# Last convolution rows and the samples' normaliser transposed on TensorE and moved by rows; GpSimd begins the sample states' transfers

## The chip, the cores and the metric

The kernel runs on one core of one Trainium2 chip. The metric is the device time of one execution in microseconds (us); for the kernel before, the median of 3 runs is 2701.5 us. The engines of the core are called PE (TensorE), ACT (ScalarE), DVE (VectorE), POOL (GpSimd) and SP (SyncE, which here only begins transfers).

## What is computed

One inference step of a single decoder layer, for one prompt of 2048 tokens and for 8 samples of one token each, model width 1024. Two mixers stand side by side: a gated delta rule (4 heads, 128 x 128 states) behind a causal convolution of width 4, and an mLSTM (4 heads, 64 x 128 matrix states with a normaliser vector and a running maximum).

```python
def _layer(x, states, params):
    h = _rmsnorm(x, norm_pre_mix)
    mix, new_states = _mixer(h, conv_buf, S0, C0, n0, m0, w_in, conv_w, ...)
    x = x + _rmsnorm(mix, norm_post_mix)
    u = jnp.square(jax.nn.relu(_rmsnorm(x, norm_pre_mlp) @ w_up))
    x = x + _rmsnorm(u @ w_down, norm_post_mlp)
    return x, new_states

# in _mixer
    (gq, gk, gv, gz, gb, ga, mq, mk, mv, mo, mi, mf) = _split(h @ w_in, IN_SPLITS)
    qkv, conv_new = _causal_conv(concatenate([gq, gk, gv]), conv_buf, conv_w)   # conv_new: the last 3 rows before the convolution
    o_gdn, S_new = _gated_delta_rule(gq, gk, gv, g, beta, S0, chunk)
    h_ml, C_new, n_new, m_new = _mlstm(mq, mk, mv, ig, lf, C0, n0, m0, chunk)
    return o @ w_out, (conv_new, S_new, C_new, n_new, m_new)

# one step for a sample
    S = exp(g) * S + k (beta * (v - exp(g) * S^T k))^T
    C = w_prev * C + p * k v^T;   n = w_prev * n + p * k
```

Besides the tokens' outputs, the new states are outputs: for the prompt the last three convolution rows (`o_pconv`, 3 x 1536), S, C, n and m; for the samples the same, among them `o_sS` (8 x 4 x 128 x 128), `o_sC` (8 x 4 x 64 x 128) and `o_sn` (8 x 4 x 64).

## The kernel before

The prompt is worked through in four segments of 512 tokens (`SEG`); the 8 samples (`NB`) ride as extra columns with segment 1 (`SS`). Activations lie channel-major: channels on the 128 partitions, tokens along the free axis. Every large product is a list of half units (`Half`): four weight blocks of 128 x 128 against four activation blocks, each in three passes (lines 195, 196, 200), 12 matmuls in all. The weights of a half unit come in one transfer of 256 KB into one of four buffers `wraw` (L171), ACT casts them to the high part `whl` (L178), DVE forms the low part (L183). PE writes into the banks `bk`, from which ACT or DVE take the results: in the up products, ACT takes them to `tB` (L1232, three buffers), which also holds the convolution's results before they are stored to `dqkv` (L309).

`play()` goes through the list `main`, which fixes the order of the half units; between them it takes steps from generators ("streams"): the mixers of a segment (`mixer`), the norms (`norm_mid`, `final`), and the samples' work (`sample_mix`, `sample_states`). A `yield` with a number says how much of the large products goes by before the next step. A scheduler then orders the instructions of each engine by its own estimate of the times, so an instruction whose inputs are early may be moved ahead of its place in the program. Each engine works in order; SP's queue is in order too, so a transfer that waits for its source or its place holds back all that SP would begin after it.

All transfers are begun by SP (`Q.dma_start`). Those that the change touches are these.

- `mixer(3)` ends by storing the prompt's states. The three last rows of the convolution lie in `halo` (128 channels x 12 tiles x 3 rows). Three transfers (L1067) move one row each, and in each the neighbours in DRAM lie on different partitions: 1536 separate words.
- `sample_mix` reads the mLSTM states of the samples, two heads at a time, into tiles `Ct` of 130 columns: 128 of C, column 128 for the normaliser n, column 129 zero. C comes in rows of 128 words, n word by word (L959: 64 partitions x 8 samples, one word each). PE then multiplies all 130 columns (L965).
- `sample_states`, a stream beside the last segment's up and down products, updates the samples' states. For each of four heads it loads S (`st_S`, 512 KB), loads the update broadcast to all partitions (`dUs`, 512 KB), multiplies and adds on POOL (L1014 to L1016), and stores `o_sS`. For each of two pairs of mLSTM heads it loads C, n and the values broadcast (`dvs`), works on all 130 columns on POOL (L1033 to L1035), and stores C and n, n again word by word (L1040). The tiles are the two buffers `xt`.

The stream `final` of segment 2 (POOL line 1306) runs before `sample_states`; the last products' sums of squares (POOL line 1124) and the last norm come after it.

Of the kernel before, what the change touches and what calls it, by code (L numbers as in the profile page):

```python
# [24 lines left out]
def program(tc, ctx, d, T):  # L25
# [48 lines left out]
    pairsum = const([128, 16], "pairsum")  # high and low part of each gate, added  # L74
# [8 lines left out]
    # the first rows, and a place for each of them normalised  # L83
# [3 lines left out]
    gain = const([128, 4, 8], "gain")  # channel-major: before and after the mixing, before and after the MLP  # L87
# [138 lines left out]
    def norm_a(xt, n, xs=None):  # L226
        """rows / rms"""
# [8 lines left out]
    def norm_b(rows, n, col, gain, halves, bank):  # L236
        """the rows of some token tiles, n tokens in all, to channel-major, times the gain, in two parts"""
# [96 lines left out]
    def a_units(s, halves, order=range(28)):  # L334
# [25 lines left out]
        if s == 0:  # L360
            # the first three of them by token halves, while the second half is being normalised
# [6 lines left out]
    def log1p_exp(L, ab, shape_n):  # L368
        """L = log1p(exp(-ab)), ab >= 0."""
# [15 lines left out]
    def gates(s):  # L385
# [32 lines left out]
        cum = sb([128, 2, 2, 16], "cum", 1)  # (cumulated | chunk total) x (g | lf)  # L418
# [69 lines left out]
    gstate = {}  # L488

    def decay(src, bias, n):  # L490
        """exp(src[c] + bias[s]) for s <= c, else 0: rows s, columns c, four heads"""
# [14 lines left out]
    def gdn_half(s, hf, D):  # L506
# [78 lines left out]
        # inverses of the 32 x 32 diagonal blocks, one block to a partition  # L585
# [62 lines left out]
        # the recurrence over chunks  # L648
# [47 lines left out]
    def out_T(s, n, on, base):  # L696
        """normalised heads, gate and gain, to channel-major scratch."""
# [84 lines left out]
    def sample_mix(s):  # L782
# [3 lines left out]
        # convolution with the buffered rows  # L786
# [39 lines left out]
        # gates, along the free axis on every partition and (last column) along the partitions  # L826
# [45 lines left out]
        # gated delta rule  # L872
# [57 lines left out]
        # mLSTM  # L930
# [21 lines left out]
        Cts = []  # L952
        for j in range(2):
            Ct = sb([128, NB, 130], "xt", 2)
            V.memset(Ct[:, :, 129:130], 0.0)
            for h2 in range(2):
                rows = slice(64 * h2, 64 * h2 + 64)
                Q.dma_start(Ct[rows, :, 0:128], d["st_C"][:, 2 * j + h2].rearrange("b k v -> k b v"))
                Q.dma_start(Ct[rows, :, 128:129], d["st_n"][:, 2 * j + h2].rearrange("b (k o) -> k b o", o=1))  # L959
# [41 lines left out]
        later.update(eg=eg, kn=kn, dU=dU, wp=wp, pp=pp, dv=dv)  # L1001
# [3 lines left out]
    def sample_states():  # L1005
        eg, kn, dU, wp, pp, dv = (later[k] for k in ("eg", "kn", "dU", "wp", "pp", "dv"))
        for h in range(4):
            St = sb([128, NB, 128], "xt", 2)
            Q.dma_start(St, d["st_S"][:, h].rearrange("b k v -> k b v"))
            Ub = sb([128, NB, 130], "xt", 2)  # L1010
            Q.dma_start(Ub[:, :, 0:128], dU[8 * h:8 * h + 8].partition_broadcast(128))
            bs = [128, NB, 128]
            yield 3
            G.tensor_tensor(St, St, eg[:, 8 * h:8 * h + 8].unsqueeze(2).broadcast_to(bs), op=ALU.mult)  # L1014
            G.tensor_tensor(Ub[:, :, 0:128], Ub[:, :, 0:128], kn[:, 8 * h:8 * h + 8].unsqueeze(2).broadcast_to(bs), op=ALU.mult)
            G.tensor_tensor(St, St, Ub[:, :, 0:128], op=ALU.add)  # L1016
            yield 4
            Q.dma_start(d["o_sS"][:, h].rearrange("b k v -> k b v"), St)
            yield 2
        for j in range(2):  # L1020
            Ct = sb([128, NB, 130], "xt", 2)
            vb = sb([128, NB, 130], "xt", 2)
            G.memset(Ct[:, :, 129:130], 0.0)
            G.memset(vb[:, :, 128:130], 1.0)
            for h2 in range(2):
                rows = slice(64 * h2, 64 * h2 + 64)
                Q.dma_start(Ct[rows, :, 0:128], d["st_C"][:, 2 * j + h2].rearrange("b k v -> k b v"))
# [546 lines left out]
```

## Time and profile before

| | before |
|---|---|
| median of 3 runs | 2701.5 us (2699.88 to 2704.51) |
| profiled execution, span from the first to the last instruction | 2703.2 us (its time; nothing is shown around it) |
| PE / DVE / ACT / POOL busy | 2605.9 / 1730.3 / 1284.0 / 412.8 us |
| packets on the DMA queue of SP | 319040, 374.57 MB |
| mean granted clock of TensorE | 0.989 |

PE is busy for 96% of the span, so the time of the kernel is the time of its matmuls and of the few gaps between them. A stretch is read by three things: how long PE is busy in it, how many matmuls it does, and which clock it was granted. The next question at a gap is which instruction ended it, and what that one had waited for.

### The profile page before, as it was taken

To read this page: it belongs to the slowest core of one execution; us is meant where nothing else is said; L and a number is where in the kernel's file an instruction comes from. 1 tells how busy PE (TensorE), PEld (TensorE's weight loads), DVE (VectorE), ACT (ScalarE), POOL (GpSimd) and SP (SyncE) were. 2 spreads that over 40 slices of the span, in tenths; PEclk is the share of its full clock that TensorE was granted. 3 is DMA by queue.
4 is the path that set the end of the run, shared out by engine and by line. 5 is a ranking of instruction groups with operands and counts; after the bars stand their busy time and mean duration, and the time that the engine had idled before them with its cause. 6 is when DMAs were issued, how large, how long until landed. Compare 5 with 4: busy or idle time off the path is not lost.

```text
span 2703.2 us, 44345 instructions
## 1 busy us (share of the span) xinstructions
PE 2605.9 (96%) x15907; PEld 2271.5 (84%) x15907; DVE 1730.3 (64%) x3508; ACT 1284.0 (48%) x3119; POOL 412.8 (15%) x470
## 2 busy tenths in 40 slices
PE   8999999999999999999799999999999999978998
PEld 6889999778888788878699999997787888766887
DVE  6765768647757557765575865587667567754445
ACT  5636457435535345644455354465363455422332
POOL 2101012311000002420000000062000004430002
PEclk9999999999999999999899999999999999999999
DMA  4444457553323245744433243454242346664222
GB/s 167 156 150 141 145 165 224 193 160 133 102 92 122 99 152 171 238 165 141 97 99 117 95 152 111 153 180 144 88 129 98 123 146 205 205 149 105 94 96 84
DMA packets 319261, 377.41 MB, mean 140 GB/s; under 512 B 53289, under 2 KB 177129, under 8 KB 319033
## 3 DMA queue, kind: packets, MB, share of 16 engines
q1 hardware_dynamic: 319040, 374.57, 44.0%
q8 instruction: 126, 2.06, 0.3%
q14 instruction: 95, 0.77, 0.1%
HBM read 314.04 MB, written 60.53 MB: 139 GB/s over the span
## 4 chain that ended last, share of the span: by engine, by line
PE 83%; DMA 6%; DVE 5%; issue 2%; ACT 2%; POOL 1%; SPq 1%; DVEq 0%; ACTq 0%; POOLq 0%
PE bk L195 25%; PE bk L196 25%; PE bk L200 24%; DVE whl L183 2%; DMA wraw<-w_o 1%; DMA xt<-x_prompt 1%; DVE nt L1197 1%; DMA wraw<-w_up 1%; DVE X L1201 1%; PE mx L563 1%; ACT whl L178 1%; DMA xt<-dO 1%; DMA dqkv<-tB 1%; PE mx L655 1%; PE mx L770 1%
## 5 line engine op out<-in xcount | busy, mean ns | idle before, releaser
L178 ACT CAST whl<-wraw 128x512 fp32r<-128x512 f32 x872 | 539.2, 620 | 972.6 <-PE bk L200 828.6
L183 DVE TENSOR_TENSOR whl<-wraw,whl 128x512 fp32r<-128x512 f32 (+1 forms) x872 | 646.5, 744 | 490.3 <-ACT whl L178 476.1
L195 PE MATMUL bk<-Y,whl 128*128 128x512 f32 (+2 forms) x2208 | 733.2, 346 | 5.7 <-ACT whl L178 3.8
L196 PE MATMUL bk<-Y,whl 128*128 128x512 f32 (+2 forms) x2208 | 731.4, 345 | 0.0
L195 PE MATMUL bk<-X,whl 128*128 128x512 f32 (+3 forms) x2024 | 659.1, 342 | 46.4 <-ACT whl L178 31.8
L196 PE MATMUL bk<-X,whl 128*128 128x512 f32 (+3 forms) x2024 | 656.6, 341 | 2.7 <-DVE X L1201 2.5
L200 PE MATMUL bk<-Y,whl 128*128 128x512 f32 (+2 forms) x2176 | 488.3, 344 | 8.8 <-DVE whl L183 8.8
L195 PEld LDWEIGHTS bk<-Y,whl 128*128 128x128 f32 x2208 | 415.8, 188 | 60.8 <-ACT whl L178 5.9
L195 PEld LDWEIGHTS bk<-X,whl 128*128 128x128 f32 x2024 | 384.1, 190 | 91.7 <-ACT whl L178 35.3
L196 PEld LDWEIGHTS bk<-Y,whl 128*128 128x128 f32 x2208 | 416.7, 189 | 50.3
L200 PE MATMUL bk<-X,whl 128*128 128x512 f32 (+3 forms) x2024 | 442.5, 339 | 8.3 <-DVE whl L183 8.2
L196 PEld LDWEIGHTS bk<-X,whl 128*128 128x128 f32 x2024 | 384.3, 190 | 47.6 <-DVE X L1201 4.1
L200 PEld LDWEIGHTS bk<-Y,whl 128*128 128x128 f32 x2176 | 358.9, 189 | 62.1 <-DVE whl L183 11.5
L200 PEld LDWEIGHTS bk<-X,whl 128*128 128x128 f32 x2024 | 326.6, 189 | 54.1 <-DVE whl L183 11.4
L1245 DVE TENSOR_TENSOR acc<-acc,bk 128x512 f32<-128x512 f32 (+2 forms) x296 | 164.1, 556 | 151.8 <-PE bk L200 147.7
L1124 POOL TENSOR_TENSOR NQ<-NQ,nt 128x256 f32<-128x256 f32 (+4 forms) x145 | 142.8, 988 | 499.0 <-ACT nt L1123 492.1
L1234 DVE TENSOR_TENSOR tB<-tB 128x512 f32<-128x512 f32 (+1 forms) x160 | 93.8, 588 | 55.7 <-ACT Y L1233 54.7
L305 DVE SCALAR_TENSOR_TENSOR tB<-tA,cw,tB 128x512 f32<-128x512 f32 x144 | 107.9, 750 | 13.7 <-ACT tB L301 11.0
L1235 DVE TENSOR_TENSOR Y<-tB,Y 128x512 fp32r<-128x512 f32 (+1 forms) x160 | 97.6, 612 | 3.2
L1232 ACT ACTIVATE tB<-bk 128x512 f32<-128x512 f32 (+1 forms) x160 | 81.7, 511 | 29.2 <-DMA dqkv<-tB 13.1
L1233 ACT ACTIVATE Y<-tB 128x512 fp32r<-128x512 f32 (+1 forms) x160 | 87.3, 549 | 4.3
L596 DVE TENSOR_TENSOR W<-xt 32x30 f32<-32x30 f32 (+14 forms) x240 | 76.2, 317 | 20.0 <-DMA xt<-dn 15.2
(380 smaller groups left out, 2456.4 us busy)
## 6 DMA issues: line engine op xcount, KB each, us to landing
wraw<-w_dn SPq DMA_DIRECT2D x264, 256.0 KB, 2.6
wraw<-w_up SPq DMA_DIRECT2D x256, 256.0 KB, 2.6
wraw<-w_a SPq DMA_DIRECT2D x224, 256.0 KB, 2.8
wraw<-w_o SPq DMA_DIRECT2D x128, 256.0 KB, 3.5
dqkv<-tB SPq DMA_DIRECT2D x48, 256.0 KB, 2.8
gb<-drb SPq DMA_DIRECT2D x32, 256.0 KB, 3.9
qk<-dqkv SPq DMA_DIRECT2D x16, 512.0 KB, 3.7
dzo<-tB SPq DMA_DIRECT2D x32, 256.0 KB, 3.2
```

The costliest lines, as they stand in the source:

```text
L178: A.copy(self.hl[:, 0], self.raw)
L183: V.tensor_tensor(lo, raw, hi.bitcast(F32), op=ALU.subtract)
L195: PE.matmul(o, lhsT=w, rhs=acts[:, k, 0, c0:c1], start=(self.first and k == 0), stop=False)
L196: PE.matmul(o, lhsT=w, rhs=acts[:, k, 1, c0:c1], start=False, stop=(self.packed and self.last and k == 3))
L200: PE.matmul(o, lhsT=w, rhs=acts[:, k, 0, c0:c1], start=False, stop=(self.last and k == 3))
L305: V.scalar_tensor_tensor(acc, pre[:, t:t + SEG], cw[:, j, t:t + 1], acc, op0=ALU.mult, op1=ALU.add)
L1124: G.tensor_tensor(total[:, c0:c1], total[:, c0:c1], sq[:, c0:c1], op=ALU.add)
L1232: A.activation(r[:, :n], p[:, :n], AF.Relu)
L1233: A.activation(sl[:, 0, c0:c1], r[:, :n], AF.Square)
L1234: V.tensor_tensor(r[:, :n], r[:, :n], r[:, :n], op=ALU.mult)
L1235: V.tensor_tensor(sl[:, 1, c0:c1], r[:, :n], sl[:, 0, c0:c1].bitcast(F32), op=ALU.subtract)
L1245: V.tensor_tensor(a, a, p[:, :c1 - c0], op=ALU.add)
```

## The change

Three edits; besides, comments are dropped, which shifts the line numbers by up to 17.

1. The prompt's last convolution rows: DVE copies `halo` into `t36` (128 x 36, tile name `hrow`), PE transposes it to 36 rows of 128 channels, ACT copies these out of PSUM into `rows36` (in the buffer `gb`), and one transfer stores 36 rows of 512 B.
2. The samples' normaliser: `sample_mix` loads n as 8 rows of 256 words (`nr`), PE transposes them into `nT` (128 x 2 x 8), which is kept, and DVE copies its columns into `Ct`. `sample_states` updates `nT` on POOL with instructions of 8 columns, and at its end PE transposes `nT` back, DVE copies the rows out, and one transfer stores `o_sn`. The tiles of the second pass have 128 columns instead of 130, so POOL's two memsets for each go.
3. In `sample_states` the transfers of the states and of the broadcasts are begun by POOL (`G.dma_start`), not by SP: 4 x 3 + 2 x 6 = 24 of them.

```diff
 # sample_mix
         pc = mx()
         Cts = []
+        nr = sb([128, 512], "on", 2)[:NB, :256]
+        Q.dma_start(nr, d["st_n"].rearrange("b h k -> b (h k)"))
+        p = mx()
+        for j in range(2):
+            PE.transpose(p[:, j * NB:(j + 1) * NB], nr[:, j * 128:(j + 1) * 128], ident[:NB, :NB])
+        nT = const([128, 2, NB], "nT")
+        V.tensor_copy(nT, p[:, 0:2 * NB].rearrange("p (a b) -> p a b", a=2))
         for j in range(2):
             Ct = sb([128, NB, 130], "xt", 2)
             V.memset(Ct[:, :, 129:130], 0.0)
+            V.tensor_copy(Ct[:, :, 128:129], nT[:, j].unsqueeze(2))
             for h2 in range(2):
                 rows = slice(64 * h2, 64 * h2 + 64)
                 Q.dma_start(Ct[rows, :, 0:128], d["st_C"][:, 2 * j + h2].rearrange("b k v -> k b v"))
-                Q.dma_start(Ct[rows, :, 128:129], d["st_n"][:, 2 * j + h2].rearrange("b (k o) -> k b o", o=1))
...
 # sample_states
         for h in range(4):
-            St = sb([128, NB, 128], "xt", 2)
-            Q.dma_start(St, d["st_S"][:, h].rearrange("b k v -> k b v"))
-            Ub = sb([128, NB, 130], "xt", 2)
-            Q.dma_start(Ub[:, :, 0:128], dU[8 * h:8 * h + 8].partition_broadcast(128))
-            bs = [128, NB, 128]
+            St = sb([128, 1040], "xt", 2)[:, :1024].rearrange("p (a b) -> p a b", a=NB)
+            G.dma_start(St, d["st_S"][:, h].rearrange("b k v -> k b v"))
+            Ub = sb([128, 1040], "xt", 2)[:, :1024].rearrange("p (a b) -> p a b", a=NB)
+            G.dma_start(Ub, dU[8 * h:8 * h + 8].partition_broadcast(128))
             yield 3
             G.tensor_tensor(St, St, eg[:, 8 * h:8 * h + 8].unsqueeze(2).broadcast_to(bs), op=ALU.mult)
...
-            Q.dma_start(d["o_sS"][:, h].rearrange("b k v -> k b v"), St)
+            G.dma_start(d["o_sS"][:, h].rearrange("b k v -> k b v"), St)
             yield 2
         for j in range(2):
...
-            G.memset(Ct[:, :, 129:130], 0.0)
-            G.memset(vb[:, :, 128:130], 1.0)
             for h2 in range(2):
                 rows = slice(64 * h2, 64 * h2 + 64)
-                Q.dma_start(Ct[rows, :, 0:128], d["st_C"][:, 2 * j + h2].rearrange("b k v -> k b v"))
-                Q.dma_start(Ct[rows, :, 128:129], d["st_n"][:, 2 * j + h2].rearrange("b (k o) -> k b o", o=1))
+                G.dma_start(Ct[rows], d["st_C"][:, 2 * j + h2].rearrange("b k v -> k b v"))
                 o0 = (2 * j + h2) * 8
-                Q.dma_start(vb[rows, :, 0:128], dv[o0:o0 + 8].partition_broadcast(64))
+                G.dma_start(vb[rows], dv[o0:o0 + 8].partition_broadcast(64))
...
             G.tensor_tensor(Ct, Ct, vb, op=ALU.add)
+            G.tensor_tensor(nT[:, j], nT[:, j], wp[:, j], op=ALU.mult)
+            G.tensor_tensor(nT[:, j], nT[:, j], pp[:, j], op=ALU.add)
             yield 4
             for h2 in range(2):
                 rows = slice(64 * h2, 64 * h2 + 64)
-                Q.dma_start(d["o_sC"][:, 2 * j + h2].rearrange("b k v -> k b v"), Ct[rows, :, 0:128])
-                Q.dma_start(d["o_sn"][:, 2 * j + h2].rearrange("b (k o) -> k b o", o=1), Ct[rows, :, 128:129])
+                G.dma_start(d["o_sC"][:, 2 * j + h2].rearrange("b k v -> k b v"), Ct[rows])
             yield 2
+        p = mx()
+        for j in range(2):
+            PE.transpose(p[:NB, j * 128:(j + 1) * 128], nT[:, j], ident)
+        nr = sb([128, 512], "on", 2)[:NB, :256]
+        V.tensor_copy(nr, p[:NB, 0:256])
+        Q.dma_start(d["o_sn"].rearrange("b h k -> b (h k)"), nr)
+        yield
 # mixer(3), at its end
             Q.dma_start(d["o_pm"], mlast)
-            for r in range(3):
-                Q.dma_start(d["o_pconv"][r].rearrange("(j p o) -> p j o", p=128, o=1), halo[:, :, r:r + 1])
+            t36 = sb([128, 36], "hrow", 1)
+            V.tensor_copy(t36[:, :].rearrange("p (r j) -> p j r", r=3), halo)
+            p = mx()
+            PE.transpose(p[:36, 0:128], t36, ident)
+            rows36 = sb([128, 512], "gb", 1)[:36, :128]
+            A.copy(rows36, p[:36, 0:128])
+            Q.dma_start(d["o_pconv"].rearrange("r (j p) -> (r j) p", p=128), rows36)
             yield
```

The order in which the engines take their instructions moves at three places. The first is SP's queue around `o_pconv`. Before, the scheduler has put the three stores far ahead of the end of `mixer(3)`, to where `halo` is complete, in the up products of segment 1; `dqkv` is the convolution's output, `gb<-drb` a broadcast of gates.

```order
525 L309 DMA dqkv_132<-tB 128x512
526 L171 DMA wraw<-w_up 128x512 x2
527 L309 DMA dqkv_132<-tB 128x512
528 L1067 DMA o_pconv<-halo 128x12x1
529 L171 DMA wraw<-w_up 128x512
530 L1067 DMA o_pconv<-halo 128x12x1 x2
531 L171 DMA wraw<-w_up 128x512
532 L502 DMA gb<-drb_151 128x512
533 L309 DMA dqkv_132<-tB 128x512
```

After the change the store needs a bank of PSUM and the buffer `gb`, which come round at the end of `mixer(3)`; it stands in SP's queue there, among the loads of the output projection's weights (`w_o`).

```order
747 L1075 DMA o_pC<-C 64x2x128
748 L1076 DMA o_pn<-C 64x2x1
749 L1075 DMA o_pC<-C 64x2x128
750 L1076 DMA o_pn<-C 64x2x1
751 L699 DMA on<-dzo_140 128x4x128
752 L171 DMA wraw<-w_o 128x512 x2
753 L1084 DMA o_pconv<-gb 36x128
754 L704 DMA dO_144<-on 128x4x128
755 L171 DMA wraw<-w_o 128x512 x2
```

So the store has moved from the middle of segment 1's up products to the first output weights of segment 3, some 220 rows later on SP. The second place is SP's queue during `sample_states`; before, loads and stores of the states stand between the weight loads.

```order
819 L1018 DMA o_sS<-xt 128x8x128
820 L1027 DMA xt<-st_C 64x8x128
821 L1028 DMA xt<-st_n 64x8x1
822 L171 DMA wraw<-w_dn 128x512
823 L1027 DMA xt<-st_C 64x8x128
824 L1030 DMA xt<-dvs 64x8x128
825 L1028 DMA xt<-st_n 64x8x1
826 L171 DMA wraw<-w_dn 128x512
827 L1030 DMA xt<-dvs 64x8x128
828 L171 DMA wraw<-w_dn 128x512 x2
829 L171 DMA wraw<-w_up 128x512
830 L1039 DMA o_sC<-xt 64x8x128
```

After the change, the same stretch of SP's queue, from the last store of `final` on, holds weight loads and one store of `o_sn`.

```order
792 L1328 DMA o_yT<-xt 128x2x512
793 L171 DMA wraw<-w_dn 128x512 x5
794 L171 DMA wraw<-w_up 128x512 x3
795 L1052 DMA o_sn<-on 8x256
796 L171 DMA wraw<-w_up 128x512 x5
797 L171 DMA wraw<-w_dn 128x512 x8
```

All that is left of the states on SP is that store. The third place is POOL, where the states' arithmetic follows the last additions of `final`; before, it is arithmetic alone.

```order
276 L1306 TENSOR_TENSOR xt<-xt,nt 128x512 x8
277 L1014 TENSOR_TENSOR xt<-xt,seg 128x1024
278 L1015 TENSOR_TENSOR xt<-xt,sy 128x8x128
279 L1016 TENSOR_TENSOR xt<-xt 128x1024
280 L1014 TENSOR_TENSOR xt<-xt,seg 128x1024
```

After, POOL also begins the transfers, in the order of the code.

```order
278 L1323 TENSOR_TENSOR xt<-xt,nt 128x512 x8
279 L1018 DMA xt<-st_S 128x8x128
280 L1020 DMA xt<-dUs 128x1024
281 L1022 TENSOR_TENSOR xt<-xt,seg 128x1024
282 L1023 TENSOR_TENSOR xt<-xt,sy 128x1024
283 L1024 TENSOR_TENSOR xt<-xt 128x1024
284 L1026 DMA o_sS<-xt 128x8x128
285 L1018 DMA xt<-st_S 128x8x128
```

POOL's 24 transfers now stand between the last addition of `final` and the first addition to the last sum of squares (L1141, which was L1124), and the first load of S can no longer begin before the last of those additions has been taken up.

## Rows read from the trace of the kernel before

**Rows 1.** The page, part 1: busy us of each engine (share) x instructions.

```profile
PE 2605.9 (96%) x15907; PEld 2271.5 (84%) x15907; DVE 1730.3 (64%) x3508; ACT 1284.0 (48%) x3119; POOL 412.8 (15%) x470
```

**Rows 2.** Timeline of PE, 1346 to 1358 us: start, us, what [idle before, releaser].

```profile
1346.47 0.58 PE L195 MATMUL bk<-X,whl 128*128 128x260 f32 x1 [12.62 <-ACT tB L1232]
...
1351.20 0.58 PE L195 MATMUL bk<-X,whl 128*128 128x260 f32 x1 [1.76 <-ACT tB L1232]
...
1353.97 0.42 PE L195 MATMUL bk<-X,whl 128*128 128x260 f32 x1
...
1355.74 0.28 PE L195 MATMUL bk<-X,whl 128*128 128x260 f32 x1
...
1357.17 1.60 PE L563 MATMUL mx<-xs 128*128 128x256 f32 x12
```

**Rows 3.** Waits, 1305 to 1352 us: us in total, times, longest us.

```profile
ACT tB L1232 <- DMA dqkv<-tB: 13.1, 1, 13.1
```

**Rows 4.** Timeline of SP, 1305 to 1352 us: start, us, what.

```profile
1315.56 1.18 SPq L1067 DMA_DIRECT2D o_pconv<-halo  x2
1317.21 12.87 SPq L171 DMA_DIRECT2D wraw<-w_up  x1
...
1330.65 0.38 SPq L309 DMA_DIRECT2D dqkv<-tB  x1
```

**Rows 5.** Chain that ended last: start, us, what.

```profile
1330.65 15.36 DMA dqkv<-tB
...
2210.09 8.67 DMA on<-dzo
```

**Rows 6.** DMA, 1305 to 1350 us: packets; an issue with KB and us to landing.

```profile
DMA packets 6412, 3.23 MB, mean 72 GB/s; under 512 B 4857, under 2 KB 4857, under 8 KB 6410
...
gb<-drb SPq DMA_DIRECT2D x1, 256.0 KB, 15.1
```

**Rows 7.** Windows: PE, PEld, DVE, ACT, POOL busy (x instructions), PEclk, DMA share, GB/s.

```profile
2325.00:2375.00 50.00, 50.00 (x216) 40.36 (x215) 33.36 (x33) 18.78 (x33) 22.76 (x13) 1.00 0.71 218
2375.00:2398.00 23.00, 20.04 (x84) 15.34 (x83) 16.41 (x14) 9.39 (x16) 13.31 (x7) 1.00 0.55 167
2398.00:2475.00 77.00, 54.32 (x216) 41.96 (x216) 31.27 (x41) 15.49 (x26) 13.58 (x9) 0.89 0.67 119
2475.00:2575.00 100.00, 100.00 (x431) 80.71 (x430) 48.47 (x72) 31.41 (x52) 0.00 (x0) 1.00 0.28 95
```

**Rows 8.** Waits, 2370 to 2460 us.

```profile
ACT whl L178 <- DMA wraw<-w_up: 40.2, 5, 16.8
...
ACT whl L178 <- DMA wraw<-w_dn: 23.0, 5, 8.8
```

**Rows 9.** DMA, 2398 to 2475 us.

```profile
DMA packets 14551, 9.20 MB, mean 119 GB/s; under 512 B 4768, under 2 KB 11859, under 8 KB 14547
...
o_sn<-xt SPq DMA_DIRECT2D x4, 2.0 KB, 11.2
```

**Rows 10.** Window around the first pass's loads of C and n.

```profile
575.00:612.00 37.00, 37.00 (x185) 29.11 (x185) 19.41 (x41) 13.38 (x26) 2.37 (x7) 1.00 0.55 157
```

**Rows 11.** Waits of SP's queue, whole span.

```profile
SPq L1018 <- POOL xt L1016: 22.2, 3, 7.7
```

**Rows 12.** Groups of DVE: 2325 to 2475 us, and the page: busy us, mean ns.

```profile
L183 DVE TENSOR_TENSOR whl<-wraw,whl 128x512 fp32r<-128x512 f32 x44 | 49.5, 1137 | 64.2 <-ACT whl L178 64.2
...
L183 DVE TENSOR_TENSOR whl<-wraw,whl 128x512 fp32r<-128x512 f32 (+1 forms) x872 | 646.5, 744 | 490.3 <-ACT whl L178 476.1
```

**Rows 13.** Timeline of PE: a transpose of 128 columns in the samples' work.

```profile
591.83 0.28 PE L899 MATMUL mx<-ident,sy 128*32 128x128 f32 x1
```

**Rows 14.** A window, and POOL's timeline before and after the states' stage.

```profile
2344.00:2445.00 101.00, 83.54 (x345) 65.10 (x344) 49.04 (x47) 27.64 (x48) 39.82 (x22) 0.95 0.67 160
...
2337.77 3.47 POOL L1306 TENSOR_TENSOR xt<-xt,nt 128x512 f32<-128x512 f32 x2 [1.14 <-DVE whl L183]
...
2670.09 0.74 POOL L1124 TENSOR_TENSOR NQ<-NQ,nt 128x256 f32<-128x256 f32 x1 [225.68 <-ACT nt L1123]
```

More of the change, by code (lines that the diff above doesn't have):

```diff
@@ L1000, in sample_mix @@
         yield
-        later.update(eg=eg, kn=kn, dU=dU, wp=wp, pp=pp, dv=dv)
+        later.update(eg=eg, kn=kn, dU=dU, wp=wp, pp=pp, dv=dv, nT=nT)
     later = {}
     def sample_states():
-        eg, kn, dU, wp, pp, dv = (later[k] for k in ("eg", "kn", "dU", "wp", "pp", "dv"))
+        eg, kn, dU, wp, pp, dv, nT = (later[k] for k in ("eg", "kn", "dU", "wp", "pp", "dv", "nT"))
+        bs = [128, NB, 128]
         for h in range(4):
-            St = sb([128, NB, 128], "xt", 2)
-            Q.dma_start(St, d["st_S"][:, h].rearrange("b k v -> k b v"))
-            Ub = sb([128, NB, 130], "xt", 2)
-            Q.dma_start(Ub[:, :, 0:128], dU[8 * h:8 * h + 8].partition_broadcast(128))
-            bs = [128, NB, 128]
+            St = sb([128, 1040], "xt", 2)[:, :1024].rearrange("p (a b) -> p a b", a=NB)
+            G.dma_start(St, d["st_S"][:, h].rearrange("b k v -> k b v"))
+            Ub = sb([128, 1040], "xt", 2)[:, :1024].rearrange("p (a b) -> p a b", a=NB)
+            G.dma_start(Ub, dU[8 * h:8 * h + 8].partition_broadcast(128))
@@ L1013, in sample_states @@
             yield 3
             G.tensor_tensor(St, St, eg[:, 8 * h:8 * h + 8].unsqueeze(2).broadcast_to(bs), op=ALU.mult)
-            G.tensor_tensor(Ub[:, :, 0:128], Ub[:, :, 0:128], kn[:, 8 * h:8 * h + 8].unsqueeze(2).broadcast_to(bs), op=ALU.mult)
-            G.tensor_tensor(St, St, Ub[:, :, 0:128], op=ALU.add)
+            G.tensor_tensor(Ub, Ub, kn[:, 8 * h:8 * h + 8].unsqueeze(2).broadcast_to(bs), op=ALU.mult)
+            G.tensor_tensor(St, St, Ub, op=ALU.add)
             yield 4
-            Q.dma_start(d["o_sS"][:, h].rearrange("b k v -> k b v"), St)
+            G.dma_start(d["o_sS"][:, h].rearrange("b k v -> k b v"), St)
@@ L1019, in sample_states @@
             yield 2
         for j in range(2):
-            Ct = sb([128, NB, 130], "xt", 2)
-            vb = sb([128, NB, 130], "xt", 2)
-            G.memset(Ct[:, :, 129:130], 0.0)
-            G.memset(vb[:, :, 128:130], 1.0)
+            Ct = sb([128, 1040], "xt", 2)[:, :1024].rearrange("p (a b) -> p a b", a=NB)
+            vb = sb([128, 1040], "xt", 2)[:, :1024].rearrange("p (a b) -> p a b", a=NB)
             for h2 in range(2):
                 rows = slice(64 * h2, 64 * h2 + 64)
-                Q.dma_start(Ct[rows, :, 0:128], d["st_C"][:, 2 * j + h2].rearrange("b k v -> k b v"))
-                Q.dma_start(Ct[rows, :, 128:129], d["st_n"][:, 2 * j + h2].rearrange("b (k o) -> k b o", o=1))
+                G.dma_start(Ct[rows], d["st_C"][:, 2 * j + h2].rearrange("b k v -> k b v"))
@@ L1029, in sample_states @@
                 o0 = (2 * j + h2) * 8
-                Q.dma_start(vb[rows, :, 0:128], dv[o0:o0 + 8].partition_broadcast(64))
-            bs = [128, NB, 130]
+                G.dma_start(vb[rows], dv[o0:o0 + 8].partition_broadcast(64))
             yield 3
```

## Prediction

> **What bounds the kernel now.** I read the page first. TensorE (PE) is busy for 2605.9 of the 2703.2 us [rows 1], so what a change can win lies in the 97.3 us in which PE does nothing, and in the stretches in which it works at the lower clock. The next views were PE's busy time in windows, PE's timeline around each gap, then the waits and SP's queue. Two places carry the word-wise transfers that the change touches, and have gaps too.
>
> Place A lies at 1346 to 1357 us. PE's rows there [rows 2] show a gap of 12.62 us ended by ScalarE's `tB` (the evacuation of an up product, L1232), a second of 1.76 us, and between and behind them matmuls of 0.42 us where later ones take 0.28: the granted clock is at its lower level. ScalarE itself had waited 13.1 us for the store `dqkv<-tB` [rows 3], which frees the third `tB` buffer. That store left SP at 1330.65 [rows 4] and took 15.36 us to land [rows 5]. Ahead of it in the same queue stand the three `o_pconv` stores, the last two from 1315.56, and behind those a weight load whose issue alone took 12.87 us [rows 4]. In this window 4857 packets are under 512 B [rows 6]; 3 x 128 x 12 = 4608 of them are the words of `o_pconv`. I take these words for the cause of the whole of A.
>
> Place B is the stage of the sample states, 2325 to 2475 us. Undisturbed, PE issues 431 matmuls in 100 us there. In the first 50 us it keeps that rate (216), although the states already move and the DMA share is 0.71. From 2375 to 2398 it does 84, from 2398 to 2475 only 216 in 77 us [rows 7]. ScalarE's weight cast (L178) waits 40.2 + 23.0 us for `wraw` [rows 8]: weights come late. From 2398 on, 4768 packets are under 512 B, of which 8 x 512 = 4096 are the words of `st_n` and `o_sn`, and an `o_sn` store takes 11.2 us to land [rows 9]. The DMA engines are about as busy as in the first 50 us (0.67), but move 119 instead of 218 GB/s [rows 7].
>
> **The sum, part by part.**
>
> *Convolution rows.* Without the three stores A goes. Its gaps are 12.62 + 1.76 us. Its two slow half units (12 matmuls each) take 2.77 us (1351.20 to 1353.97, and the one before it counted alike), a third 1.77 (to 1355.74), and the next at full clock 1.43 [rows 2]; that is 2 x 1.34 + 0.34 = 3.02 us more than at full clock. A is worth 12.62 + 1.76 + 3.02 = 17.4 us. In its place come a VectorE copy, one transpose, one ScalarE copy and one store of 36 rows, much later, among the first `w_o` loads. There the store `dO<-on`, SP's next instruction, waits anyway for `on<-dzo`, which lands 8.67 us after 2210.09 [rows 5], so the wait of the `o_pconv` store for its ScalarE copy is covered until about 2219. Were that cover gone, the loads behind it would be late by at most a half unit of 2.8 us.
>
> *Word loads of the first pass.* The four `st_n` loads of `sample_mix` cost PE nothing: it is busy for all 37 us around them [rows 10]. Their removal is worth 0. On SP the new load of 8 rows stands ahead of the last two `st_C` loads, for which the same products wait.
>
> *Sample states.* At 4.31 matmuls per us, 84 matmuls are worth 19.5 of 23 us, and 216 are worth 50.1 of 77 [rows 7]. So PE lost 3.5 + 26.9 = 30.4 us, slow clock included (0.89 in the last stretch). The words go altogether. The 24 other transfers move to GpSimd's queue, which takes a second thing away: SP issues in order, and its stores of the states waited 22.2 us for GpSimd's additions, with weight loads behind them [rows 11]. What stays is 12 x 0.5 + 12 x 0.25 = 9 MB of rows of 512 B and more, on the same DMA engines, and GpSimd's arithmetic, beside which VectorE's weight split (L183) takes 1137 ns against 744 in the mean of the program [rows 12]. The 3.5 us before 2398 were lost without any word transfer, so some of it can stay: between 0 and, if each of the three pairs of groups lost as much, 10 us. I take 2, as the first 50 us of the same traffic lost nothing.
>
> Here a rule speaks against half of the change. The Trainium skill, "DMA: Bandwidth & Descriptors", section "Issuing engines are not separate DMA queues", says that transfers begun by several engines interleave on the same 16 DMA engines, and that beginning them elsewhere saves only the issuing time. By that rule the move to GpSimd wins nothing, the 3.5 us stay, and the sum below would be 42.4 instead of 43.9.
>
> *Added work.* Five transposes at 0.28 us [rows 13] are 1.4 us on PE. The store `o_sn` now waits on SP for a VectorE copy behind the second `nT` transpose; behind it stand weight loads that lose two half units of a lead of about four. I price that at 0.5 us, between 0 and one half unit of 12 / 4.31 = 2.8.
>
> Sum: 17.4 + 30.4 - 2 - 1.4 - 0.5 = 43.9 us. The profiled execution lasted 2703.2 us; 2703.2 - 43.9 = 2659.3. The median of the runs, 2701.5, is 1.7 below it, so I expect 2657.6, say **2658**.
>
> *GpSimd's issues.* No row of this trace shows a DMA issued by GpSimd. The nearest rows bound it: SP issues a store of 256 KB in 0.38 us (the row at 1330.65 in [rows 4]), and GpSimd walks a tile of 128 x 1024 words in 39.82 / 18 = 2.2 us, four short memsets counted in [rows 14]. I take 2.2, since it is the same engine going over the same rows. 24 x 2.2 = 53 us lengthen the states' stage. What hides it: after the states GpSimd sat idle for 225.68 us until its next addition at 2670.09 [rows 14], and no other engine waits for the states.
>
> **Rivals.**
>
> *B is the volume, not the words.* Then PE goes on losing its 30.4 us while the states move, and only A is won: 2703.2 - 17.4 + 1.9 - 1.7 = 2686. For it: 3.5 us lost before the first word, and an almost unchanged DMA share. Against it: 0.71 of the share and 218 GB/s without a lost matmul [rows 7]. Chance 0.12.
>
> *A has another cause,* such as the broadcast `gb<-drb`, whose landing took 15.1 us [rows 6]. Then only B is won: 2703.2 - 30.4 + 3.9 - 1.7 = 2675. Against it: one transfer of 256 KB in a window that 4608 words fill. Chance 0.04.
>
> *GpSimd becomes the bound (the other side).* Its first state load can start when its last addition of the norm before is done, 17.4 us earlier than now, at 2337.77 + 3.47 - 17.4 = 2323.8; its first addition to the last sum of squares is wanted at 2670.1 - 43.9 = 2626.2 [rows 14]. Of these 302 us the states' stage takes 101 as it is, 40 of work and 61 of waiting for transfers [rows 14]. The rest, 201 us, is 8.4 us for each of 24 issues. Above that every us costs 24 at the end, since the last additions, norms and stores follow; from (201 + 43.9 + 5.4) / 24 = 10.4 us each the kernel is slower than before by over 0.2%. At 12 us each it would be 2658 + 24 x 3.6 = 2744. For it: GpSimd and VectorE hinder each other [rows 12], and VectorE is busy for 33.36 of 50 us [rows 7]; were issuing shut out for all of that, 2.2 us would become 6.6. Against it: 6.6 is still below 8.4. Chance 0.05. The Trainium skill, "SBUF — State Buffer", section "SBUF: two separate sides", names the trap: VectorE's two-port copies lock GpSimd out while it writes descriptors. VectorE's largest group here is tensor-tensor [rows 12], and by the rule only copies and their like do it, so the chance stays small.
>
> **How the numbers follow.** The forecast has a chance of 0.79, the rivals 0.12, 0.04 and 0.05. The forecast's own range comes from its bounds: nothing left of B and nothing for the transposes and `o_sn` gives 2654; 10 us left and 2.8 for `o_sn` give 2668; with some 3 us each way for the scatter of the runs (2699.9 to 2704.5) it is 2651 to 2671. To leave out no more than 2 in 10, the range takes in the second rival and a partly won B: 2650 to 2680. 0.2% (5.4 us) is about what a measurement of this kernel tells from no change. Faster: 0.79 + 0.12 + 0.04 less 0.01 for gains given back on GpSimd, 0.94; same 0.02; slower 0.04.
>
> **What the profile after should show.** No gap and no low clock at 1330 to 1360; `dqkv<-tB` landing in about 3 us there. From 2300 to 2430 some 2 us of PE idle and 4.3 matmuls per us throughout; 8700 fewer packets under 512 B; a second queue with the states' transfers; no SP wait for GpSimd's additions of states. GpSimd's stage from about 2324 to 2480, well before 2626. The prediction is wrong if weights still come late beside GpSimd's transfers (L178 waiting for `wraw`), or if GpSimd's first addition after the states waits for its own queue.

## The result and the profile after

The changed kernel takes 2653.61 us (median of 4 runs, 2652.65 to 2654.62) against 2701.58 us before (4 runs, 2699.88 to 2704.51). The ratio is 0.9818, with a 95% interval of 0.9804 to 0.9832: 48.0 us less, where 43.5 us had been forecast (2658). The profiled execution spans 2652.3 us.

The page of the kernel after: busy time of each engine (answers to [rows 1]), the packets and the DMA queues.

```profile
PE 2599.9 (98%) x15912; PEld 2268.5 (86%) x15912; DVE 1727.5 (65%) x3513; ACT 1283.5 (48%) x3120; POOL 433.3 (16%) x494
...
DMA packets 292221, 377.40 MB, mean 142 GB/s; under 512 B 42325, under 2 KB 147785, under 8 KB 291993
...
q1 hardware_dynamic: 289312, 365.13, 44.2%
q0 software_dynamic: 2688, 9.44, 1.3%
```

PE's five instructions more are the transposes. POOL's 24 more are the transfers (the four memsets that went and the four short updates of `nT` that came cancel out); these make a queue of their own, q0. The bytes are the same as before to 0.01 MB; the packets under 512 B are 10,964 fewer (53,289 before).

Windows of the kernel after: the stretch of place A, then those of [rows 7] (columns as there).

```profile
1305.00:1360.00 55.00, 55.00 (x444) 54.13 (x442) 41.17 (x98) 36.85 (x112) 4.94 (x6) 1.00 0.36 111
2325.00:2375.00 50.00, 50.00 (x218) 40.17 (x217) 28.18 (x31) 20.16 (x36) 27.78 (x19) 1.00 0.63 202
2375.00:2398.00 23.00, 23.00 (x100) 18.61 (x99) 11.94 (x16) 5.59 (x10) 13.45 (x10) 1.00 0.72 203
2398.00:2475.00 77.00, 77.00 (x332) 62.08 (x331) 45.03 (x57) 25.75 (x43) 15.35 (x13) 1.00 0.43 120
2475.00:2575.00 100.00, 100.00 (x431) 80.71 (x430) 48.11 (x71) 31.41 (x52) 0.00 (x0) 1.00 0.30 95
```

PE is busy for every microsecond of both places, at the full clock, and issues 332 matmuls in 77 us, the rate of the undisturbed last row. The states' traffic is in these windows as before, at 202 and 203 GB/s.

**Where the time came from.** But for the transposes, PE executes the same instructions in both kernels, at both places in the same order, so the start of one instruction can be compared directly. Four of them, in the timeline of PE after, bound two stages: from the first `mx<-ident,qk` before place A to `mx<-xs` behind it, and from the twelve `mx<-ones,NQ` before the sample states to the four at the end.

```profile
1312.36 0.60 PE L520 MATMUL mx<-ident,qk 128*128 128x128 f32 x4
...
1336.18 1.00 PE L563 MATMUL mx<-xs 128*128 128x256 f32 x7
...
2291.13 1.50 PE L1153 MATMUL mx<-ones,NQ 128*128 128x2 f32 x12
...
2630.89 0.50 PE L1153 MATMUL mx<-ones,NQ 128*128 128x2 f32 x4
```

In the timeline of PE before, the second of the four starts at 1357.17 (last row of [rows 2]); the others are these.

```profile
1315.64 0.60 PE L520 MATMUL mx<-ident,qk 128*128 128x128 f32 x4
...
2311.45 1.50 PE L1136 MATMUL mx<-ones,NQ 128*128 128x2 f32 x12
...
2681.68 0.50 PE L1136 MATMUL mx<-ones,NQ 128*128 128x2 f32 x4
```

Stage A fell from 41.53 to 23.82 us (17.71 less), stage B from 370.23 to 339.76 (30.47 less). The spans differ by 50.9 us; the other 2.7 lie elsewhere, 2.1 of them before 54 us, where nothing was changed. These two lengths are a finer ruler than the time of a run: stage A is within 0.1 us of 23.82 in all nine kernels of this study that don't put words there, and stage B within 0.1 us of 339.76 in the four that change only the last convolution rows, while the runs of one kernel scatter by 2 to 13 us.

Waits of SP's queue from 2300 to 2480 us after (answers to [rows 11]):

```profile
SPq L171 <- DVE whl L183: 139.0, 63, 5.8
SPq L1328 <- POOL xt L1323: 10.2, 4, 4.4
...
SPq L1052 <- DVE on L1051: 1.3, 1, 1.3
```

The first line is no trouble: a weight load waiting for its buffer means that weights are ahead. What SP still waits for POOL are stores of a norm's output, not of states.

POOL after: groups of its DMA issues from 2320 to 2425 us (busy us, mean ns), and in its timeline the first and last issue and the next addition (answers to [rows 14]).

```profile
L1026 POOL DMA_DIRECT2D o_sS<-xt x4 | 3.8, 954 | 1.2 <-POOL xt L1024 1.2
L1018 POOL DMA_DIRECT2D xt<-st_S x4 | 3.8, 946 | 0.0
L1045 POOL DMA_DIRECT2D o_sC<-xt x4 | 2.9, 734 | 0.6 <-POOL xt L1039 0.6
L1033 POOL DMA_DIRECT2D xt<-st_C x4 | 2.8, 696 | 0.0
L1020 POOL DMA_DIRECT2D xt<-dUs x4 | 2.3, 566 | 12.9 <-DMA o_sS<-xt 10.0 <-DMA o_yT<-xt 2.9
L1035 POOL DMA_DIRECT2D xt<-dvs x4 | 2.1, 537 | 6.9 <-DMA o_sC<-xt 4.2 <-DMA o_sS<-xt 2.7
```
```profile
2321.18 1.12 POOL L1018 DMA_DIRECT2D xt<-st_S  x1
...
2420.72 1.47 POOL L1045 DMA_DIRECT2D o_sC<-xt  x2 [0.29 <-POOL xt L1039]
2619.30 0.74 POOL L1141 TENSOR_TENSOR NQ<-NQ,nt 128x256 f32<-128x256 f32 x1 [197.12 <-ACT nt L1140]
```

The 24 issues took 17.7 us in all, 0.74 each, and the stage ended 197 us before GpSimd was wanted again.

### The profile page after: what moved, and what is told of

Read it like the earlier page. It is cut to its first block, busy times and chain, and to the rows that moved or that the text cites. A ratio compares the mean times of both kernels' runs of the same rounds, so it can differ in the third digit from the quotient of the medians.

```text
span 2652.3 us, 44344 instructions
## 1 busy us (share of the span) xinstructions
PE 2599.9 (98%) x15912; PEld 2268.5 (86%) x15912; DVE 1727.5 (65%) x3513; ACT 1283.5 (48%) x3120; POOL 433.3 (16%) x494
## 3 DMA queue, kind: packets, MB, share of 16 engines
q0 software_dynamic: 2688, 9.44, 1.3%
## 4 chain that ended last, share of the span: by engine, by line
PE 88%; DVE 4%; DMA 4%; issue 2%; ACT 1%; POOL 0%; SPq 0%; DVEq 0%; ACTq 0%; POOLq 0%
PE bk L195 26%; PE bk L196 26%; PE bk L200 26%; DMA wraw<-w_o 1%; DVE whl L183 1%; DVE nt L1214 1%; DMA xt<-x_prompt 1%; DVE X L1218 1%; DMA xt<-dO 1%; PE mx L563 1%; PE mx L655 1%; PE mx L770 1%; PE mx L680 1%; PE mx L681 1%; PE mx L747 1%
## 5 line engine op out<-in xcount | busy, mean ns | idle before, releaser
L183 DVE TENSOR_TENSOR whl<-wraw,whl 128x512 fp32r<-128x512 f32 (+1 forms) x872 | 636.3, 732 | 447.5 <-ACT whl L178 433.3
L196 PEld LDWEIGHTS bk<-Y,whl 128*128 128x128 f32 x2208 | 416.9, 189 | 50.4
L1141 POOL TENSOR_TENSOR NQ<-NQ,nt 128x256 f32<-128x256 f32 (+4 forms) x145 | 143.3, 991 | 470.5 <-ACT nt L1140 464.1
L305 DVE SCALAR_TENSOR_TENSOR tB<-tA,cw,tB 128x512 f32<-128x512 f32 x144 | 108.0, 750 | 13.6 <-ACT tB L301 9.3
L596 DVE TENSOR_TENSOR W<-xt 32x30 f32<-32x30 f32 (+14 forms) x240 | 76.2, 317 | 22.3 <-DMA xt<-dn 17.5
```

The costliest lines, as they stand in the source:

```text
L183: V.tensor_tensor(lo, raw, hi.bitcast(F32), op=ALU.subtract)
L196: PE.matmul(o, lhsT=w, rhs=acts[:, k, 1, c0:c1], start=False, stop=(self.packed and self.last and k == 3))
L305: V.scalar_tensor_tensor(acc, pre[:, t:t + SEG], cw[:, j, t:t + 1], acc, op0=ALU.mult, op1=ALU.add)
L1141: G.tensor_tensor(total[:, c0:c1], total[:, c0:c1], sq[:, c0:c1], op=ALU.add)
```

## The experiments

Each kernel is told with its lengths of stages A and B beside those of the changed kernel (23.82 and 339.76 us), and the median with its ratio to the kernel before (timed anew beside each group of kernels, 2700.3 to 2702.6 us, which the ratio goes by). Stage lengths are differences of the starts named above, in one profiled execution.

| kernel | A, us | B, us | median, us | ratio (95%) |
|---|---|---|---|---|
| before | +17.71 | +30.47 | 2701.58 | 1 |
| changed | 0 | 0 | 2653.61 | 0.9818 (0.9804 to 0.9832) |
| conv_rows | 0.00 | +26.96 | 2686.36 | 0.9938 (0.9917 to 0.9958) |
| rows_sp | 0.00 | +9.25 | 2665.14 | 0.9861 (0.9844 to 0.9879) |
| words_g | 0.00 | +4.65 | 2660.30 | 0.9845 (0.9822 to 0.9868) |
| conv_g | +14.54 | -0.09 | 2670.85 | 0.9885 (0.9865 to 0.9905) |
| conv_third | 0.00 | +0.01 | 2654.43 | 0.9835 (0.9818 to 0.9851) |
| conv_third_g | +0.07 | 0.00 | 2652.34 | 0.9826 (0.9806 to 0.9846) |
| conv_two_g | +6.93 | -0.10 | 2663.25 | 0.9863 (0.9848 to 0.9878) |
| burst_b | -0.01 | +10.54 | 2666.74 | 0.9880 (0.9857 to 0.9903) |
| stores_g | 0.00 | +11.07 | 2665.83 | 0.9874 (0.9859 to 0.9889) |
| sp_wait | 0.00 | +19.95 | 2672.47 | 0.9896 (0.9879 to 0.9912) |
| words_g_wait | -0.01 | +21.83 | 2674.01 | 0.9897 (0.9880 to 0.9913) |
| oyt_g | 0.00 | +1.17 | 2660.70 | 0.9853 (0.9838 to 0.9868) |

**Is place A the words of `o_pconv`? (conv_rows)** The kernel before with only this:

```diff
-            for r in range(3):
-                Q.dma_start(d["o_pconv"][r]..., halo[:, :, r:r + 1])
+            t36 = sb([128, 36], "hrow", 1)
...
+            Q.dma_start(d["o_pconv"].rearrange("r (j p) -> (r j) p", p=128), rows36)
```

> The kernel before with o_pconv alone by rows. Theory (the words of o_pconv are the whole of place A): 17.4 to 18.0 us less than before, 2683.5 to 2684; no gap of PE at 1330 to 1360, dqkv<-tB lands in about 3 us, and the states' stage loses its 30 us as before. Rival (place A belongs to another transfer there, such as gb<-drb): within 3 us of before, the gap stays.

Stage A took 23.82 us, the length of the changed kernel to the hundredth: the 17.71 us are the words' alone, and the broadcast `gb<-drb` is no cause of them. Stage B kept 26.96 us of its loss.

**Do the words hurt through SP's queue, or through the DMA engines? (conv_g)** The changed kernel with the three word stores at their old place, begun by GpSimd:

```diff
-            Q.dma_start(d["o_pconv"].rearrange("r (j p) -> (r j) p", p=128), rows36)
+            for r in range(3):
+                G.dma_start(d["o_pconv"][r].rearrange("(j p o) -> p j o", p=128, o=1), halo[:, :, r:r + 1])
```

> The changed kernel with o_pconv by words at its old place, its three stores begun by GpSimd. Theory 1 (words hold the DMA engines): PE's gap at 1330 to 1360 is back, 10 to 18 us slower than the changed kernel, 2664 to 2672. Theory 2 (only the order in SP's queue): within 3 us, 2651 to 2657, dqkv<-tB lands in 3 to 6 us.

Stage A lost 14.54 us. DMA issues of conv_g from 1305 to 1360 us (KB each, median us to landing), and the gaps in PE's timeline:

```profile
wraw<-w_up SPq DMA_DIRECT2D x12, 256.0 KB, 13.6
...
o_pconv<-halo POOLq DMA_DIRECT2D x3, 6.0 KB, 25.1
```
```profile
1330.21 0.55 PE L195 MATMUL bk<-X,whl 128*128 128x260 f32 x1 [3.30 <-ACT tB L1244]
1342.49 0.58 PE L195 MATMUL bk<-X,whl 128*128 128x260 f32 x1 [4.33 <-ACT tB L1244]
1347.22 0.58 PE L195 MATMUL bk<-X,whl 128*128 128x260 f32 x1 [1.76 <-ACT tB L1244]
```

18 KB of words on a queue of their own make weights of 256 KB land in 13.6 us in the median (2.9 in the changed kernel's A, below), so the words hold the DMA engines that all queues share. Taking them off SP's queue gave back 3.2 of 17.7 us.

**How does the cost grow with the number of words? (conv_third, conv_third_g, conv_two_g)** One third of the words from SP, one third from GpSimd, two thirds from GpSimd, the rest by rows:

```diff
-            Q.dma_start(d["o_pconv"].rearrange("r (j p) -> (r j) p", p=128), rows36)
+            Q.dma_start(d["o_pconv"][1:3].rearrange("r (j p) -> (r j) p", p=128), rows36[12:36])
+            Q.dma_start(d["o_pconv"][0].rearrange("(j p o) -> p j o", p=128, o=1), halo[:, :, 0:1])
```

> The changed kernel with one of the three rows of o_pconv (1536 words) stored by words from SP at its old place, the other two by rows. Theory (PE loses what the words take beyond the weights' lead of some four half units, 11 us): a burst a third as long, some 5 us, is covered, 0 to 3 us slower than the changed kernel at 1330 to 1360. Rival (each word costs PE its share): a third of place A, about 6 us slower.

> The same third of o_pconv by words, begun by GpSimd. Theory (burst beyond the lead): 0 to 2 us slower than the changed kernel, the store landing in some 8 us (25.1 for three). Rival (each word costs PE its share whichever queue it is in): 5 us, a third of the 15 us that all three cost from GpSimd.

> The changed kernel with two of the three rows of o_pconv (3072 words) stored by words from GpSimd at the old place, the third by rows. Three rows from GpSimd landed in 25.1 us and cost some 15 us at 1330 to 1360, one row cost nothing. Theory (what lands after a lead of some 10 us costs, the rest is covered): landing in 16 to 17 us, a cost of 5 to 8 us. Rival (a threshold of another kind, such as a third store that finds no place): nothing, 0 to 2 us, or all of it, 13 to 17.

Nothing from either queue for 1536 words, 6.93 us for 3072, 14.54 for 4608. The DMA issues of conv_two_g in the same stretch:

```profile
o_pconv<-halo POOLq DMA_DIRECT2D x2, 6.0 KB, 19.7
```

The landing was longer than I had worked out (16 to 17 us), the cost as the theory had it: what lands after the weights' lead costs PE, and what lands within it is free. The landing less the cost is 19.7 - 6.93 = 12.8 us for two rows and 25.1 - 14.54 = 10.6 us for three, near a lead of four half units (4 x 2.78 = 11.1 us, an estimate from [rows 7]).

**Is place A special? (burst_b)** The same 4608 words, begun by GpSimd in the sample states instead (behind a copy of `halo` that waits for the first state's load):

```diff
+            if h == 0:
+                z = sb([128, 4], "st", 4)[:, 0:1]
+                G.tensor_scalar(z, St[:, 0, 0:1], 0.0, None, op0=ALU.mult)
+                hc = sb([128, 36], "hrow", 1)[:, :].rearrange("p (j r) -> p j r", r=3)
+                G.tensor_tensor(hc, halo, z.unsqueeze(2).broadcast_to([128, 12, 3]), op=ALU.add)
+                for r in range(3):
+                    G.dma_start(d["o_pconv"][r]..., hc[:, :, r:r + 1])
```

> The changed kernel with the 4608 words of o_pconv stored by GpSimd in the states' stage, behind the first state's load (a copy of halo that waits for that load is stored), instead of by rows at the end of the mixer. Theory (a burst of words longer than the weights' lead costs PE some 15 us wherever weights stream, on whatever queue): the states' stage 8 to 17 us longer than in the changed kernel, weights landing in over 10 us. Rival (place A is special, since the store dqkv<-tB holds a buffer there): 0 to 3 us longer.

10.54 us were lost in stage B, in the shortest of its four executions. DMA issues from 2315 to 2400 us, and PE's waits there:

```profile
wraw<-w_up SPq DMA_DIRECT2D x13, 256.0 KB, 15.0
...
o_pconv<-hrow POOLq DMA_DIRECT2D x3, 6.0 KB, 19.1
```
```profile
PE bk L195 <- ACT whl L178: 8.3, 1, 8.3
```

In the changed kernel the same loads of `w_up` land in 2.7 us in the median. No buffer of `dqkv<-tB` stands here: place A is not special, the burst suffices at this second place too.

**Words or queue, in the sample states? (rows_sp, words_g)** The changed kernel with all 24 transfers begun by SP; and the changed kernel with the normaliser moved by words again, but from GpSimd:

```diff
-            G.dma_start(St, d["st_S"][:, h].rearrange("b k v -> k b v"))
+            Q.dma_start(St, d["st_S"][:, h].rearrange("b k v -> k b v"))
...
```
```diff
+                G.dma_start(Ct[rows, :, 128:129], d["st_n"][:, 2 * j + h2].rearrange("b (k o) -> k b o", o=1))
...
+                G.dma_start(d["o_sn"][:, 2 * j + h2].rearrange("b (k o) -> k b o", o=1), Ct[rows, :, 128:129])
```

> The changed kernel with the states' transfers begun by SP in place of GpSimd, all by rows. Theory 1 (the words are the whole of place B, the queue that begins the transfers is worth nothing): within 3 us of the changed kernel, 2651 to 2657. Theory 2 (SP's waits for GpSimd's additions, 22 us before, hold weight loads back): 5 to 30 us slower than the changed kernel, 2659 to 2684, with L178 waiting for wraw behind an SP wait for GpSimd.

> The changed kernel with the normaliser by words again, its 12 word transfers of the states' stage begun by GpSimd with the others (the first pass stays by rows). Theory 1 (words keep the 16 DMA engines from the weights, whatever queue they are in): 15 to 30 us slower than the changed kernel, 2669 to 2684. Theory 2 (words hurt only as what stands ahead of the weights in SP's own queue): within 3 us of the changed kernel, 2651 to 2657, with o_sn taking some 10 us on a queue of its own.

Rows from SP lose 9.25 us, as the second theory had it, words from GpSimd 4.65 (in eight transfers, not the twelve of the expectation), both together (conv_rows) 26.96, neither 0. Waits of SP's queue in rows_sp, 2300 to 2480 us, and DMA issues of words_g, 2320 to 2480 us:

```profile
SPq L1026 <- POOL xt L1024: 29.6, 4, 7.9
SPq L1045 <- POOL xt L1039: 16.2, 2, 8.5
```
```profile
xt<-st_n POOLq DMA_DIRECT2D x4, 2.0 KB, 11.6
o_sn<-xt POOLq DMA_DIRECT2D x4, 2.0 KB, 11.9
```

In words_g each of the word transfers takes as long as before ([rows 9]: 11.2 us), but they come in issues of 512 words, at most 2048 close together, and by the dose found at place A (nothing for 1536, 6.93 us for 3072) that is nearly covered. Both theories of words_g had expected otherwise (nothing, or 15 us and more).

**Which instruction on SP holds the weights? (stores_g)** The states' loads on SP, only the stores on GpSimd:

```diff
-            G.dma_start(St, d["st_S"][:, h].rearrange("b k v -> k b v"))
+            Q.dma_start(St, d["st_S"][:, h].rearrange("b k v -> k b v"))
...
             G.dma_start(d["o_sS"][:, h].rearrange("b k v -> k b v"), St)
```

> The changed kernel with the states' loads begun by SP and only their stores by GpSimd. Theory (SP is held by the stores that wait for GpSimd's additions, as with all of them on SP, where the states' stage took 9.3 us longer): 0 to 3 us longer in that stage than the changed kernel. Rival (SP is held by loads that wait for a free buffer): 5 to 10 us longer, as with all of them on SP.

My theory of the stores fell: 11.07 us were lost. The waits of SP's queue show that with two buffers the next load waits for the same addition, or for the store behind it to land:

```profile
SPq L1018 <- POOL xt L1024: 21.9, 3, 7.6
SPq L1020 <- DMA o_sS<-xt: 16.0, 3, 5.7
SPq L1033 <- POOL xt L1024: 7.0, 1, 7.0
```

**The wait, or the bytes in the queue? (sp_wait)** The changed kernel with six SP stores of one row of 512 B, each waiting for an addition of GpSimd:

```diff
+            Q.dma_start(probe[h:h + 1], St[0:1, 0, :])
             G.dma_start(d["o_sS"][:, h].rearrange("b k v -> k b v"), St)
...
+            Q.dma_start(probe[4 + j:5 + j], Ct[0:1, 0, :])
```

> The changed kernel with six stores more, of one row of 512 B each, begun by SP at the places where it would begin the states' stores: each waits on SP for GpSimd's addition and moves next to nothing into a spare DRAM tile. Theory (what SP's queue costs is that weight loads stand behind instructions that wait for GpSimd): the states' stage 5 to 10 us longer than in the changed kernel, as with all transfers on SP (9.3 us) or all loads on SP (11.2 us). Rival (it is the states' bytes in the same queue as the weights, or SP's time for issuing them): 0 to 2 us longer.

3 KB cost 19.95 us, twice what the theory had. Waits of SP's queue and its timeline:

```profile
SPq L1027 <- POOL xt L1025: 47.3, 4, 14.7
SPq L1045 <- POOL xt L1041: 19.8, 2, 10.1
```
```profile
2335.22 0.25 SPq L1027 DMA_DIRECT2D probe<-xt  x1
...
2352.15 0.25 SPq L1027 DMA_DIRECT2D probe<-xt  x1
2352.50 1.76 SPq L171 DMA_DIRECT2D wraw<-w_up  x4
2356.79 0.33 SPq L171 DMA_DIRECT2D wraw<-w_dn  x1
2368.28 0.25 SPq L1027 DMA_DIRECT2D probe<-xt  x1
```

That is the mechanism in five rows: between two waits stand 5 weight loads, which are worth 5 x 2.78 = 13.9 us of PE (12 matmuls at 4.31 per us, [rows 7]), but the waits come 16 to 17 us apart for the four states and 19 to 20 for the two pairs, GpSimd's pace. SP can't go on to the sixth. In rows_sp, where the pace is 13 to 16 us, less is lost. From the first to the last of the six waits it is 88.7 us with 24 loads, worth 66.8: 21.9 us short, and 19.95 lost. The same count, from the first to the last wait for GpSimd in the other timelines of SP, worked out after these runs and so an estimate: rows_sp 12.9 short (71.4 us, 21 loads) and 9.25 lost, stores_g 12.6 (62.8, 18) and 11.07, words_g_wait (next) 26.7 (99.1, 26) and 21.83. In each the loss is 1.5 to 4.9 us less than the shortfall, which is within the weights' lead estimated above.

**Do the two costs multiply? (words_g_wait)** words_g and sp_wait in one.

```diff
+            Q.dma_start(probe[h:h + 1], St[0:1, 0, :])
...
+            Q.dma_start(probe[4 + j:5 + j], Ct[0:1, 0, 0:128])
```

> Words of the normaliser begun by GpSimd (4.65 us more in the states' stage than the changed kernel) and six SP stores of one row that wait for GpSimd's additions (19.95 us more) together. If the two costs are of two kinds, they add: 24 to 26 us more in that stage. Theory for what was lost before (26.96 us with o_pconv by rows, where words on GpSimd alone cost 4.65 and the waits alone 9.25): words make GpSimd's work late, some 11 us to land each time, and SP then waits for GpSimd as much longer, so the two together cost more than the sum, 28 to 40 us.

21.83 us, less than either theory had it. Waits of SP's queue:

```profile
SPq L1026 <- POOL xt L1024: 40.5, 4, 12.1
SPq L1046 <- POOL xt L1044: 23.8, 2, 12.6
```

64.3 us of waiting against 67.1 in sp_wait: the words did not add to SP's waits, but the last two now stand 28.0 us apart, with 7 loads between them (19.2 us and 5 in sp_wait). The sum of the two costs was not exceeded, so this alone doesn't explain why words and states on SP lose 26.96 us where the parts lose 9.25 and 4.65. The trace of conv_rows shows a part of it, in a wait of GpSimd from 2320 to 2480 us:

```profile
POOL xt L1024 <- DMA o_sn<-xt: 13.8, 1, 13.8
```

GpSimd takes up the last pair only when the word stores have landed, and SP's last two waits stand 28.1 us apart, with 5 loads between them (15.8 us and 4 in rows_sp). By the count above conv_rows is 20.9 us short (85.0 us, 23 loads), 8 more than rows_sp. That leaves 6 us and more beside the waits, more than the 4.65 that the words cost on GpSimd's queue: in conv_rows weights land in 6.1 to 6.3 us from 2390 to 2460 us, in rows_sp in 2.6 to 2.7. Whether that rest is the common queue, or weights issued in bunches just behind the words, stays open.

**A further gain? (oyt_g)** The last norm's output stores, for which SP still waits, begun by GpSimd as well:

```diff
             if not end:
-                Q.dma_start(dst[j0:j0 + k, :, c0:c1]...
+                G.dma_start(dst[j0:j0 + k, :, c0:c1]...
```

> The changed kernel with the output stores of the last norm (o_yT, but for those at the end) begun by GpSimd, which makes the rows they store, in place of SP, which waits up to 4.4 us for each. Theory (a queue of weights pays only for waits longer than its lead of some 10 us): nothing to gain, within 3 us of the changed kernel, 2650 to 2657. Rival (every wait of SP for GpSimd costs PE): the 18 us that SP waits there come back in part, 2640 to 2649.

No gain, and slower than either had it, 2660.70 us. Stages A and B are nearly as they were (+0.00 and +1.17 us). In the profiled execution, 11.8 us longer than that of the changed kernel, 8.0 us are lost before 1060 us, where PE's order is that of the changed kernel, and words_g and rows_sp, which change nothing before the sample states, lie 10.6 and 5.4 us behind at that point; some 3.5 us come from 1090 to 1210 us, where PE's order differs. So it is not shown that the edit costs time. No kernel here beats the changed one beyond its interval; conv_third_g (2652.34) is the same within it.

## Why the prediction came out right, step by step

**Convolution rows.** Forecast 17.4 us, measured 17.71. The step was right in place, cause and size. Its path, the store `dqkv<-tB` held in SP's queue behind the words and a weight load of 12.87 us of issue, was only part of it: the words jam the engines, not only that queue (conv_g). `dqkv<-tB` lands in 3.3 us in the median of the program after, and no engine waits for it in this stretch. DMA of the kernel after, 1305 to 1350 us (answers to [rows 6]):

```profile
wraw<-w_up SPq DMA_DIRECT2D x12, 256.0 KB, 2.9
...
gb<-drb SPq DMA_DIRECT2D x2, 256.0 KB, 3.8
```

`gb<-drb` falls from 15.1 to 3.8 us with the words gone: it was a victim.

**Sample states.** Forecast 30.4 - 2 - 0.5 us less two of the five transposes, measured 30.47 with all of that in it. The 2 us for what might stay were 0 (PE busy throughout), the 0.5 us for `o_sn` too: SP waits 1.3 us there and PE stays busy. These terms and the 1.4 us of transposes, which no stage shows apart, are 3.9 of the 4.5 us by which the forecast was too high.

**The sharing of that gain.** The prediction gave the 30.4 us to the words first and named SP's waits as a second thing, worth 1.5 us in its sum (43.9 against 42.4). The runs put it the other way: rows from SP alone cost 9.25 us, words from GpSimd alone 4.65, and from 26.96 us moving the issue takes 22.3 away, moving by rows 17.7. It had read one of four lines; the other waits of SP for GpSimd in this stage before, 2300 to 2480 us, make it 50.4 us instead of the 22.2 of [rows 11]:

```profile
SPq L1039 <- POOL xt L1035: 10.9, 1, 10.9
SPq L1039 <- POOL xt L1023: 9.2, 1, 9.2
SPq L1018 <- POOL xt L1023: 8.1, 1, 8.1
```

The sum was right all the same because it was read from what PE lost, and the change removes both causes; for either edit alone this sharing would have forecast wrongly.

**The rule against it.** The Trainium skill, "DMA: Bandwidth & Descriptors", section "Issuing engines are not separate DMA queues", has transfers interleave on the same engines whoever begins them. On that, conv_g agrees: 4608 words from GpSimd cost nearly as much. That beginning them elsewhere saves only the issuing time, the measurement contradicts here: rows_sp is 9.25 us longer in B, and sp_wait loses 19.95 us with stores that SP issues in 0.25 us each. What it saves is the wait of an in-order queue.

**Volume as the cause.** That rival fell: the same bytes in the same windows, and no lost matmul.

**GpSimd as the bound.** It had 2.2 us for each issue, and 8.4 us as the limit; measured 0.54 to 0.95 us, and a stage from 2321 to 2422 us, not 2480. The second page of the Trainium skill that the prediction cites, "SBUF — State Buffer", "SBUF: two separate sides", warned of VectorE locking GpSimd out; no issue took over 1.2 us with VectorE busy for 28.18 of 50 us, so this trace shows none of it. VectorE's split, 1137 ns in this stretch before [rows 12], is still above its mean in the program after, 732 ns; that GpSimd's additions beside it are the reason is not tested:

```profile
L183 DVE TENSOR_TENSOR whl<-wraw,whl 128x512 fp32r<-128x512 f32 x54 | 47.5, 882 | 36.9 <-ACT whl L178 36.8
```

**Packets.** Forecast 8700 fewer under 512 B, found 10,964: I had left out the 2048 words of the first pass, and some 200 stay unexplained. Those words cost PE nothing, as forecast.

## What to carry to other kernels

A transfer of 4-byte words is priced by how long it keeps the DMA engines from the stream that PE lives on, less that stream's lead: at place A 1536 words were free and a burst of 4608 was not, and another queue gave back only 3.2 of 17.7 us. The eight pieces of words_g still cost 4.65 us; whether a burst split and spaced further would be free was not tested. An in-order issuing queue that feeds PE should hold no instruction that waits for a slow engine, load or store, however few bytes it moves: count the weight loads that stand between two such waits and compare their worth with the time from wait to wait. Let the engine that makes the data begin its transfers, if it has the time: here 17.7 us of issuing against 197 us of idle time.

## What was unexpected in the hardware

18 KB in words kept the DMA engines at 4 to 46 GB/s for ten slices of 2.1 us in burst_b, while their share of busy time rose to 0.7 to 0.9 in the second half of them: here the share says nothing of what they move. On GpSimd's queue the same states' rows are recorded as 2688 packets for 9.44 MB, some 3.5 KB each; on SP's, rows_sp shows 13,600 packets under 2 KB from 2320 to 2480 us where words_g has 1617.
